# Three transpose banks for part of the band attention, a deferred output norm, and row factors kept in SBUF

## The chip, the core and the metric

The kernel runs on one core of a Trainium2 chip. The metric is the time of one execution in device microseconds (us). A core has a matrix engine (TensorE; PE in the profile, with its weight loads as PEld), a vector engine (VectorE; DVE), an activation engine (ScalarE; ACT), a general engine (GpSimd; POOL) and the queue from which this kernel issues its DMAs (SyncE; SP). Each engine takes its instructions in one fixed order, which is set when the program is built. Matrix products land in PSUM, in banks of 128 x 512 float32 values; working tiles lie in SBUF.

## The reference

One layer of a streaming encoder on 2048 prompt tokens and 32 sample tokens, all in float32. Both attention groups read the same projected input, and their outputs meet in one output projection:

```python
qa, ka, va, qb, kb, vb = split_proj(rmsnorm(hp, g_attn[i]), w_in[i])
oa = diff_attn_prompt(qa, ka, va, t5_table, lam)      # group A: 4 heads, two maps, chunk-causal
ob = band_attn_prompt(qb, kb, vb, band_table[i])      # group B: 8 heads, own chunk and 8 before it
hp = hp + merge(oa, ob, subln_g[i], out_norm_b[i], w_out[i], lam_init)
hp = ffn_ple(hp, p_prompt[i], g_mlp[i], w_up[i], w_down[i], w_ple_gate[i], w_ple_proj[i])

def merge(oa, ob, subln_g, out_norm_b, w_out, lam_init):
    oa = rmsnorm(oa, subln_g, SUBLN_EPS) * (1.0 - lam_init)
    ob = rmsnorm(ob.reshape(B, T, WIDTH_B), out_norm_b)
    return jnp.concatenate([oa.reshape(B, T, WIDTH_A), ob], axis=-1) @ w_out
```

What the change touches is the projection, the band attention (group B) and `merge`: the norm over the 512 columns of `ob`, and the product with `w_out`.

## The kernel before

**Precision.** A float32 operand is split into a high and a low part, and a product is made of three matmuls (`mm3`, lines 219 to 221). The splits are ACT's (high part, line 181) and POOL's or DVE's (low part, lines 166, 176, 187). A weight tile of 512 KB is read, split and then used by a group of 24 matmuls: 8 slices of the contraction, three matmuls each.

**Blocks.** The 2080 tokens form four blocks: 0 to 2 of 512, and 3 of 544 with the sample tokens, which is worked in two halves of 272. Blocks 0 and 1 go through projection, attention, output projection and MLP ahead of blocks 2 and 3.

**Projections** (`proj`). For group B (`grp` 1) and group A (`grp` 0): values per 128 tokens (tile `vps`, 24 matmuls 256 wide, evicted by ACT, line 427), then queries and keys per 128 columns (tile `qps`, 24 matmuls 512 or 272 wide, evicted by DVE, lines 475 and 480). Before, their PSUM tiles go round three banks: `mm` is a ring of two banks of the pool `mz` and one of the pool `mmx`.

**Band attention** (`attn_b`). A head's queries are taken 128 at a time; I call one such tile a band step. With all 640 keys it has four score matmuls in two banks (`sb`, line 804), the bias and maximum on DVE (line 807), the exponential and the scaling on ACT (lines 812, 814, with DVE's small steps 811 and 813 between), five transposes of the weights (`tpb`, line 826) into two tiles of PSUM, their eviction as high and low part by ACT and DVE (`pb`, lines 834, 835), and, once for two steps, the product with the values (`ob`, line 856: six matmuls, evicted at lines 859 to 861). The heads are called in four sets, `JB`: pairs of 256 queries (0, 1), (2, 3), (4, 5) and (6, 7, 8), eight heads each; the first two sets are the first half, `JB[: len(JB) // 2]`. Steps of the first set have fewer keys and two score matmuls each. Banks: two for scores (`ps_s`), two for transposes (`ps_t`), one for outputs (`ps_o`).

**Output norm and projection.** The attention outputs go to memory (`oT`) and come back. `onorm` reads the four group B slices of a block, squares and adds them (ACT lines 875, 877; POOL), and `colnorm2` makes the row factors r from them (two `css` matmuls, ACT lines 1050 to 1052, DVE 1053 to 1056) and stores them in memory (`rB`). `oload` reads r back and all eight slices (`raw_o`, tile `oraw`, a ring of `self.nt` buffers tagged `tmp`), multiplies four of them by gain and r (line 902) and splits them (`oact`). `outproj` then runs eight groups of 24 matmuls (`ops`), one for each 128 output columns, and adds the input (`hd`, line 926).

**Order.** Code order is a priority. A scheduler places each instruction on its engine when it can run by its own estimate, so that matmuls of the band attention stand between those of the projections. `weave` and `weave2` issue one generator's pieces between another's steps. Before, the norms of blocks 0 and 1 are issued within the group A projection of blocks 2 and 3 (`ONP`: from step 28 on), and block 1's `oload` within block 0's output projection, one slice for each of its eight steps (`OW`).

Of the kernel before, what the change touches and what calls it, by code (L numbers as in the profile page):

```python
# [13 lines left out]
F32 = mybir.dt.float32  # L14
# [4 lines left out]
PSUM = bass.MemoryType.PSUM  # L19

P = 128
# [13 lines left out]
BLK = 544  # L35
# [7 lines left out]
HALVES = [(0, 1), (2, 3)]  # L43
# [29 lines left out]
GS = 3  # L73
OW = 1
# [4 lines left out]
ONP = (28, 1, 6)  # L79
ONQ = (8, 1, 1)  # L80
PW = 272


def drain(gen):
    for _ in gen:
        pass


def weave2(main, sides, at):
    n = 0  # L90
    for _ in main:
        for i, side in enumerate(sides):
            if n in (at[0] + i * at[1], at[0] + i * at[1] + at[2]):
                next(side, None)
        n += 1
    for side in sides:
        drain(side)


def weave(main, side, step, i=0, n=1):  # L100
    for _ in main:
        if i % step == 0:
            for _ in range(n):
                next(side, None)
        i += 1
    drain(side)
# [37 lines left out]
class Kern:  # L144
# [14 lines left out]
    def pool_tt(self, out, a, b, op):  # L159
        nc = self.nc  # L160
        if len(out.shape) == 2:
            n = out.shape[1]
            m = -(-n // PW)
            for i in range(m):
# [700 lines left out]
        self.dma(t, self.oT[:, k, t0 : t0 + n])  # L865
        return t

    def onorm(self, b, wk, ps, tag, dst):
        nc = self.nc
        n, t0 = BN[b], 512 * b  # L870
        sq = wk.tile([P, BLK], F32, tag="acc", bufs=2, name="sqacc")[:, :n]
        for k in range(4, 8):
            raw = self.raw_o(wk, k, t0, n)
            if k == 4:
                nc.scalar.activation(sq, raw, AF.Square)
            else:
                nc.scalar.activation(raw, raw, AF.Square)
                self.pool_tt(sq, sq, raw, ALU.add)
        yield from self.colnorm2(sq, b, 1.0 / 512, wk, ps, tag, dst, [])

    def oload(self, b, wk, up, out):
        nc = self.nc
        n, t0 = BN[b], 512 * b
        if isinstance(up, tuple):
            oact = up[0].tile([P, 8, n], F32R, tag="h", name="oact")
            oact = [
                [oact[:, k] for k in range(8)],
                [up[1].tile([P, up[1].aw], F32R, tag="u", name="ou") for _ in range(8)],
            ]
        elif up.whole:  # L890
            oact = [up.tile([P, 8, up.aw], F32R, tag="act", name="oact") for _ in range(2)]
            oact = [[t[:, k, :n] for k in range(8)] for t in oact]
        else:
            oact = [[up.tile([P, up.aw], F32R, tag="u", name="ou")[:, :n] for k in range(8)] for _ in range(2)]
        out[b] = oact
        for k in range(8):
            if k == 4:
                r = wk.tile([P, BLK], F32, tag="r", bufs=2, name="rb")[:, :n]
                self.dma(r, self.rB[:, t0 : t0 + n])
            raw = self.raw_o(wk, k, t0, n)  # L900
            if k >= 4:
                nc.vector.scalar_tensor_tensor(
                    raw, raw, self.g_b[:, k - 4 : k - 3], r, op0=ALU.mult, op1=ALU.mult
                )
            self.split(oact[0][k], oact[1][k], raw, "act", "dve")
            yield
# [473 lines left out]
    def run(self):  # L1380
        tc, nc, a = self.tc, self.nc, self.a
        with ExitStack() as top:

            def opened(stack, name, bufs, space=None, side="left"):
                kw = {} if space is None else {"space": space}
                return stack.enter_context(
                    tc.tile_pool(name=name, bufs=bufs, side=side, reuse_waits="tile", **kw)
                )
# [8 lines left out]
            mm = opened(top, "mm", MM, PSUM)  # L1397
            mmx = ExitStack()
            mm0 = mz = mm
            mm = Rings((mz, "mm"), (mz, "mm"), (opened(mmx, "mmx", 1, PSUM), "mm"))  # L1400
            tp = mm
            psx = ExitStack()
            ps_s = opened(psx, "pss", 4 - MM, PSUM, "right")
            ps_t = opened(psx, "pst", 2, PSUM, "right")
            ps_o = opened(psx, "pso", 1, PSUM, "right")
# [3 lines left out]
            sg = opened(s12, "sg", 2)  # L1409
            self.rb = {}  # L1410
            with ExitStack() as x:
                pp = opened(x, "pp0", 3, side="right")
                wv = opened(x, "wv0", 1, side="right")
                acts = {b: self.actpair() for b in HALVES[0]}
# [20 lines left out]
            pp = opened(ppx, "pp", 1)  # L1435
            self.rawp = Rings((self.wp, "wr"), (opened(ppx, "wr3", 1), "wr"))
            with ExitStack() as x:
                wk = opened(x, "setup", 1, side="right")
# [11 lines left out]
            def lifted(gen):  # L1450
                while True:
                    with tc.high_priority(tc.tile_snap_priority() - mark):
                        done = next(gen, self) is self
                    if done:
                        return
                    yield
# [5 lines left out]
            self.rows(3, sg)  # L1462
            bx = ExitStack()
            bp = opened(bx, "b", 1, side="right")
            for js in JB[: len(JB) // 2]:
                self.attn_b(js, bp, ps_s, ps_t, ps_o)
            weave(self.proj((2,), 1, acts, sg, mm), lifted(self.prep(3, acts, pp, mm, "mm")), 3)
            ppx.close()
            self.rawp = Rings((self.wp, "wr"))
            self.caches(sg, tp)  # L1470
            drain(self.proj((3,), 1, acts, sg, mm))
            wqx = ExitStack()
            wq = opened(wqx, "wq", 1, side="right")
            for js in JB[len(JB) // 2 :]:
                self.attn_b(js, bp, ps_s, ps_t, ps_o)

            def proj_a():
                yield from self.proj(HALVES[1], 0, acts, sg, mm, gs=range(GS))
                for b in HALVES[1]:
                    yield from self.proj((b,), 0, acts, sg, mm, vs=(), gs=range(GS, 4))  # L1480

            weave2(proj_a(), [self.onorm(b, wq, mm, "mm", self.rB) for b in HALVES[0]], ONP)
            s12.close()
            self.small = False
            sq_ = ExitStack()
            actq = Sized(opened(sq_, "actq", 2), 512, True)
            oa = {}
            drain(self.oload(0, wq, actq, oa))
            wqx.close()
            bx.close()  # L1490
            wk = opened(sq_, "wk", 1)
            fk = opened(sq_, "fk", 1)
            hq = opened(sq_, "hq", 1)
            uq = Sized(opened(sq_, "uq", 8), 512)
            self.qpool = opened(sq_, "ak", 1)
            mz = mm
# [7 lines left out]
            acc, cn, st = {}, {}, {}  # L1504
# [3 lines left out]
                yield from self.cnorm(b, wk, act, cn)  # L1508

            acc = {b: [] for b in range(4)}  # L1510
            weave(self.outproj(0, wk, oa[0], mm, acc[0]), self.oload(1, wk, (hq, uq), oa), 1, 0, OW)
            weave(self.outproj(1, wk, oa[1], mm, acc[1]), norms(0, actq, mm), 1, 1)
            up = Sized(opened(top, "uh", 20, side="right"), BLK)
            oxs = ExitStack()
# [7 lines left out]
            for b in HALVES[0]:  # L1522
# [4 lines left out]
                h = hload(hq, 512, b)  # L1527
# [10 lines left out]
            mm = mm0  # L1538
# [8 lines left out]
            wk = opened(top, "wk4", 1, side="right")  # L1547
# [5 lines left out]
            with ExitStack() as x:  # L1553
# [3 lines left out]
                g = self.outproj(3, wk, oa[3], md, acc[3])  # L1557
# [9 lines left out]
            h = hload(hh[0], BLK, 0)  # L1567
            g = self.gate(0, h, up, None, md, wk, made[0], pT)
# [7 lines left out]
            h = box[0]  # L1576
# [3 lines left out]
            g = self.gate(2, h, up, None, md, wk)  # L1580
# [8 lines left out]
            h = box[0]  # L1589
            weave(m, f, 1)  # L1590
            g = self.gate(3, h, up, cs, md)
# [67 lines left out]
```

## Time and profile before

| | before |
|---|---|
| median of three runs | 3063.79 us (3062.14 to 3065.21) |
| the profiled execution | 3069.65 us |
| its span, first to last instruction | 3067.9 us |
| TensorE busy | 2947.2 us (96%) |
| mean granted TensorE clock | 0.985 |
| scores of the band attention (`sb`) on TensorE | from 525.0 to 1231 us |
| last matmul of the projections (`qps`) starts | 773.1 us |
| first matmul of the output projection (`ops`) starts | 825.5 us |

The profile is of one execution. Busy shares count an engine's instructions; matmuls overlap, so a group's busy time is more than the time it takes on a full engine. A wait is the idle time of an engine just ahead of an instruction, with the engine and tile that ended it.

### The profile page before, as it was taken

Reading aid. Unit: us, or ns where it says so; the run is one execution under the profiler, and the core shown is the slowest. Engines: PE = TensorE matmul, PEld = TensorE weight load, DVE = VectorE, ACT = ScalarE, POOL = GpSimd, SP = SyncE. Lnnn points to the kernel's source line nnn. Section 1 sums busy time; section 2 is a strip of 40 time slices with the busy share of each in tenths; the row PEclk is TensorE's granted clock in tenths of the full one; section 3 lists DMA queues with packets and bytes.
Section 4 is the critical chain, followed back from the end, with each engine's and each line's share of the span. In section 5 each row is a group of like instructions: output and inputs, shape, how many; then the busy total and the mean of one; then the engine's idle time right before and its main releaser. Section 6 shows DMA issues by size and latency. Waiting matters only on the chain. (4 is left out here: it accounts for less than half of the span.)

```text
span 3067.9 us, 50404 instructions
## 1 busy us (share of the span) xinstructions
PE 2947.2 (96%) x17409; PEld 2599.0 (85%) x17409; DVE 1830.6 (60%) x4233; ACT 1746.5 (57%) x3234; POOL 1887.9 (62%) x2509
## 2 busy tenths in 40 slices
PE   7999999899789999999999999999899999999997
PEld 6788889899677888888888888879798888999997
DVE  5156554654655555566666565545677885577664
ACT  5256554765666666566666565554555545555455
POOL 3467775324146544656655565777688888787774
PEclk9999999999899999999999999999999999999999
DMA  9878866976687554455655543347433446333331
GB/s 310 250 222 245 241 221 211 262 228 211 190 248 241 147 148 131 145 155 172 198 149 155 150 128 125 118 148 249 136 131 117 148 151 231 122 101 112 102 99 57
DMA packets 298119, 529.54 MB, mean 173 GB/s; under 512 B 36668, under 2 KB 161632, under 8 KB 297864
## 3 DMA queue, kind: packets, MB, share of 16 engines
q1 hardware_dynamic: 297864, 526.32, 55.6%
q8 instruction: 138, 2.26, 0.3%
q14 instruction: 117, 0.96, 0.1%
HBM read 425.19 MB, written 104.97 MB: 173 GB/s over the span
## 5 line engine op out<-in xcount | busy, mean ns | idle before, releaser
L176 POOL TENSOR_TENSOR wl<-wr,wh 128x256 fp32r<-128x256 f32 x648 | 492.8, 792 | 270.2 <-ACT wh L181 230.7
L181 ACT ACTIVATE piece<-wr 128x512 fp32r<-128x512 f32 x406 | 245.8, 625 | 290.4 <-PE ups L220 133.3
L176 POOL TENSOR_TENSOR piece<-wr,piece 128x256 fp32r<-128x256 f32 x404 | 338.0, 863 | 92.3 <-ACT piece L181 85.2
L181 ACT ACTIVATE wh<-wr 128x1024 fp32r<-128x1024 f32 x228 | 240.5, 1055 | 190.8 <-PE ups L220 45.9
L166 POOL TENSOR_TENSOR wl<-wr,wh 128x256 fp32r<-128x256 f32 x264 | 202.9, 799 | 208.4 <-ACT wh L181 202.6
L219 PE MATMUL dps<-uh,piece 128*128 128x272 f32 (+1 forms) x768 | 247.0, 325 | 8.3 <-ACT piece L181 5.0
L221 PE MATMUL dps<-uh,piece 128*128 128x272 f32 (+1 forms) x768 | 247.3, 325 | 1.1 <-POOL piece L166 0.9
L220 PE MATMUL dps<-ul,piece 128*128 128x272 f32 (+1 forms) x768 | 248.1, 324 | 0.1
L166 POOL TENSOR_TENSOR piece<-wr,piece 128x256 fp32r<-128x256 f32 x280 | 235.1, 872 | 18.9 <-ACT piece L181 15.4
L219 PE MATMUL ups<-cs,piece 128*128 128x256 f32 (+1 forms) x864 | 246.2, 285 | 0.0
L221 PE MATMUL ups<-cs,piece 128*128 128x256 f32 (+1 forms) x864 | 246.1, 285 | 0.0
L220 PE MATMUL ups<-cs,piece 128*128 128x256 f32 (+1 forms) x864 | 245.9, 285 | 0.0
L219 PE MATMUL qps<-aH,wh 128*128 128x512 f32 (+1 forms) x640 | 226.9, 355 | 2.0 <-DVE ql L475 2.0
L220 PE MATMUL qps<-aL,wh 128*128 128x512 f32 (+1 forms) x640 | 227.9, 356 | 0.0
L221 PE MATMUL qps<-aH,wl 128*128 128x512 f32 (+1 forms) x640 | 226.5, 354 | 0.0
L1112 DVE TENSOR_TENSOR h<-h,dps 128x512 f32<-128x512 f32 x256 | 173.5, 682 | 80.2 <-PE dps L221 77.0
L638 ACT ACTIVATE e<-e,nm 128x128 f32<-128x128 f32 (+16 forms) x136 | 157.2, 1156 | 108.5 <-DVE nm L636 108.0
L1155 DVE TENSOR_TENSOR h<-h,dps 128x272 f32<-128x272 f32 (+1 forms) x384 | 189.0, 514 | 42.9 <-PE dps L221 42.3
L219 PE MATMUL dps<-uh,wh 128*128 128x512 f32 x512 | 205.7, 402 | 0.6 <-DVE h L1112 0.6
L219 PE MATMUL ups<-cH,wh 128*128 128x512 f32 x512 | 202.5, 396 | 0.0
L221 PE MATMUL ups<-cH,wl 128*128 128x512 f32 x512 | 202.2, 395 | 0.1
L220 PE MATMUL ups<-cL,wh 128*128 128x512 f32 x512 | 202.0, 394 | 0.0
(307 smaller groups left out, 9234.0 us busy)
## 6 DMA issues: line engine op xcount, KB each, us to landing
wr<-w_up SPq DMA_DIRECT2D x128, 512.0 KB, 3.5
wr<-w_down SPq DMA_DIRECT2D x128, 512.0 KB, 3.6
v<-vSa SPq DMA_DIRECT2D x64, 512.0 KB, 4.6
q<-qS SPq DMA_DIRECT2D x128, 256.0 KB, 5.2
wr<-w_qk SPq DMA_DIRECT2D x50, 512.0 KB, 5.2
ka<-kS SPq DMA_DIRECT2D x32, 512.0 KB, 7.1
wr<-w_out SPq DMA_DIRECT2D x32, 512.0 KB, 4.8
wr<-w_ple_gate SPq DMA_DIRECT2D x32, 512.0 KB, 3.5
```

The source lines that it names most:

```text
L166: nc.gpsimd.tensor_tensor(out[:, sl], a[:, sl], b[:, sl], op=op)
L176: nc.gpsimd.tensor_tensor(out[:, sl], a[:, sl], b[:, sl], op=op)
L181: nc.scalar.activation(hi, raw, AF.Copy)
L219: nc.tensor.matmul(ps, lh, rh, start=start and i == 0, stop=False)
L220: nc.tensor.matmul(ps, lh, rl, start=False, stop=False)
L221: nc.tensor.matmul(ps, ll, rh, start=False, stop=stop and i == n - 1)
L638: nc.scalar.activation(row, row, AF.Exp, bias=nmx, accum_out=z[:nr, m : m + 1])
L1112: nc.vector.tensor_tensor(hv, hv, ps, op=ALU.add)
L1155: nc.vector.tensor_tensor(hv, hv, ps, op=ALU.add)
```

## The change

Four edits, in one diff:

- The band attention's first half (sets 0 and 1) transposes into a ring of three banks: the two of `ps_t` and the one of `mmx`. From there on the projections of blocks 2 and 3, and the preparation of block 3, use the two banks of `mz` alone.
- Only block 0's norm is still issued within the group A projection. Block 1's is issued within block 0's output projection: its first piece after step 3, its second after step 5 (`O1`, `O2`). It reads its four slices in one DMA into a tile of the pool `hq`, and adds them up in one of `uq`, not in the `tmp` and `acc` rings.
- Block 1's `oload` begins after step 5 and issues three slices for each step (`O3`), in place of one from step 0 on.
- r of blocks 0 and 1 stays in the SBUF tile that `colnorm2` made; it isn't stored to `rB` and read back. Blocks 2 and 3 are as before.

```diff
+O1, O2, O3 = 3, 5, 3
-    def onorm(self, b, wk, ps, tag, dst):
+    def onorm(self, b, wk, ps, tag, dst, out=None, room=None):
         nc = self.nc
         n, t0 = BN[b], 512 * b
-        sq = wk.tile([P, BLK], F32, tag="acc", bufs=2, name="sqacc")[:, :n]
+        if room is None:
+            sq = wk.tile([P, BLK], F32, tag="acc", bufs=2, name="sqacc")[:, :n]
+        else:
+            room, sq = room
+            sq = sq.tile([P, sq.aw], F32, tag="u", name="sqacc")[:, :n]
+            room = room.tile([P, 8, n], F32, tag="h", name="oraws")[:, :4]
+            self.dma(room, self.oT[:, 4:8, t0 : t0 + n])
         for k in range(4, 8):
-            raw = self.raw_o(wk, k, t0, n)
+            raw = self.raw_o(wk, k, t0, n) if room is None else room[:, k - 4]
...
-        yield from self.colnorm2(sq, b, 1.0 / 512, wk, ps, tag, dst, [])
+        yield from self.colnorm2(sq, b, 1.0 / 512, wk, ps, tag, dst, [] if out is None else out)
-    def oload(self, b, wk, up, out):
+    def oload(self, b, wk, up, out, r=None):
...
-            if k == 4:
+            if k == 4 and r is not None:
+                r = r.pop()
+            elif k == 4:
                 r = wk.tile([P, BLK], F32, tag="r", bufs=2, name="rb")[:, :n]
                 self.dma(r, self.rB[:, t0 : t0 + n])
...
-            mm = Rings((mz, "mm"), (mz, "mm"), (opened(mmx, "mmx", 1, PSUM), "mm"))
+            third = opened(mmx, "mmx", 1, PSUM)
+            mm = Rings((mz, "mm"), (mz, "mm"), (third, "mm"))
...
+            tb = Rings((ps_t, "tp"), (ps_t, "tp"), (third, "mm"))
             for js in JB[: len(JB) // 2]:
-                self.attn_b(js, bp, ps_s, ps_t, ps_o)
-            weave(self.proj((2,), 1, acts, sg, mm), lifted(self.prep(3, acts, pp, mm, "mm")), 3)
+                self.attn_b(js, bp, ps_s, tb, ps_o)
+            weave(self.proj((2,), 1, acts, sg, mz), lifted(self.prep(3, acts, pp, mz, "mm")), 3)
...
-            drain(self.proj((3,), 1, acts, sg, mm))
+            drain(self.proj((3,), 1, acts, sg, mz))
...
-                yield from self.proj(HALVES[1], 0, acts, sg, mm, gs=range(GS))
+                yield from self.proj(HALVES[1], 0, acts, sg, mz, gs=range(GS))
                 for b in HALVES[1]:
-                    yield from self.proj((b,), 0, acts, sg, mm, vs=(), gs=range(GS, 4))
-            weave2(proj_a(), [self.onorm(b, wq, mm, "mm", self.rB) for b in HALVES[0]], ONP)
+                    yield from self.proj((b,), 0, acts, sg, mz, vs=(), gs=range(GS, 4))
+            ro = {b: [] for b in HALVES[0]}
+            weave2(proj_a(), [self.onorm(0, wq, mm, "mm", None, ro[0])], ONP)
...
-            drain(self.oload(0, wq, actq, oa))
+            drain(self.oload(0, wq, actq, oa, ro[0]))
...
-            weave(self.outproj(0, wk, oa[0], mm, acc[0]), self.oload(1, wk, (hq, uq), oa), 1, 0, OW)
+            g = self.onorm(1, wk, mm, "mm", None, ro[1], (hq, uq))
+            for i, _ in enumerate(self.outproj(0, wk, oa[0], mm, acc[0])):
+                if i in (O1, O2):
+                    next(g, None)
+                if i == O2:
+                    g = self.oload(1, wk, (hq, uq), oa, ro[1])
+                if i >= O2:
+                    for _ in range(O3):
+                        next(g, None)
+            drain(g)
```

The scheduler makes a new order of this. On TensorE, at the end of the projections, before (names end in a buffer number; `kbt_6457` holds the keys of the last head of band set 1, `x2` is two equal matmuls):

```order
L219 MATMUL qps_12209<-aH_4781,wh_12171 128x272
L220 MATMUL qps_12209<-aL_4782,wh_12171 128x272
L221 MATMUL qps_12209<-aH_4781,wl_12172 128x272
L1046 MATMUL css_12244<-sh_11920,ones_r_118 128x512
L1047 MATMUL css_12244<-sl_11921,ones_r_118 128x512
L804 MATMUL sb_6468<-kbt_6457,q_6460 128x320 x2
L804 MATMUL sb_6472<-kbt_6457,q_6460 128x320 x2
L856 MATMUL ob_6355<-pb_6305,vbt_6192 128x512 x4
L856 MATMUL ob_6355<-pb_6305,vbt_6192 128x2x128
L826 MATMUL tpb_6381<-ident_111,eb_6330 128x128 x4
```

Nothing but band steps follows, up to the second head of band set 2 (`kbt_8433`), where the output projection begins:

```order
L804 MATMUL sb_8541<-kbt_8433,q_8436 128x320 x2
L804 MATMUL sb_8545<-kbt_8433,q_8436 128x320 x2
L826 MATMUL tpb_8456<-ident_111,eb_8403 128x128 x4
L219 MATMUL ops_16133<-oact_12272,wh_16124 128x512
L219 MATMUL ops_16185<-oact_12272,wh_16176 128x512
```

Changed, the same place on TensorE (`kbt_8705` holds the keys of the fourth head of band set 2):

```order
L222 MATMUL qps_12186<-aH_4781,wl_12149 128x272
L1055 MATMUL css_12221<-sh_11920,ones_r_118 128x512
L1056 MATMUL css_12221<-sl_11921,ones_r_118 128x512
L805 MATMUL sb_8716<-kbt_8705,q_8708 128x320 x2
L805 MATMUL sb_8720<-kbt_8705,q_8708 128x320 x2
L857 MATMUL ob_8603<-pb_8553,vbt_8440 128x512 x4
L857 MATMUL ob_8603<-pb_8553,vbt_8440 128x2x128
L827 MATMUL tpb_8629<-ident_111,eb_8578 128x128 x4
L857 MATMUL ob_8603<-pb_8553,vbt_8440 128x2x128
L827 MATMUL tpb_8636<-ident_111,eb_8578 128x128
L220 MATMUL ops_16095<-oact_12236,wh_16086 128x512
L220 MATMUL ops_16134<-oact_12236,wh_16125 128x512
```

What moved: 16 band steps (176 score matmuls stand ahead of the last `qps` before, 240 now, four for a step) went from behind the projections into them. Between the last `qps` and the first `ops` stand 48 score matmuls, 12 band steps, before, and four, one band step, now.

On SP, the DMA queue, at block 1's `oload` within block 0's output projection, before (`hd` is the input that the output projection adds, `hS` its result):

```order
L157 DMA oraw_16262<-oT_87 128x512
L157 DMA hd_16275<-x_t 128x512
L157 DMA wr_16455<-w_out 128x1024
L157 DMA hS_88<-hd_16275 128x512
L157 DMA oraw_16308<-oT_87 128x512
L157 DMA hd_16321<-x_t 128x512
L157 DMA wr_16503<-w_out 128x1024
L157 DMA hS_88<-hd_16321 128x512
L157 DMA oraw_16356<-oT_87 128x512
```

Changed:

```order
L158 DMA oraw_16370<-oT_87 128x512
L158 DMA oraw_16374<-oT_87 128x512
L158 DMA wr_16546<-w_out 128x1024
L158 DMA oraw_16378<-oT_87 128x512
L158 DMA wr_16598<-w_out 128x1024
L158 DMA hd_16391<-x_t 128x512
L158 DMA vbt_8984<-vSb_86 128x8x128
L158 DMA oT_87<-t1_8711 64x512
L158 DMA hS_88<-hd_16391 128x512
L158 DMA oraw_16424<-oT_87 128x512
L158 DMA oraw_16428<-oT_87 128x512
```

What moved: the eight reads stood one to a step of the output projection, and stand now in pairs and threes towards its end. The reads of `rB` and the stores to it, two each, are gone, and block 1's norm reads once instead of four times: seven DMAs fewer in all. Every compute engine has the same instructions as before, in another order.

## Prediction

> **What bounds the kernel now.** I read the page's first part, then the busy time of each engine by stretches, then TensorE's waits in the stretches that have any.
>
> ```profile
> PE 2947.2 (96%) x17409; PEld 2599.0 (85%) x17409; DVE 1830.6 (60%) x4233; ACT 1746.5 (57%) x3234; POOL 1887.9 (62%) x2509
> ```
>
> TensorE is busy for 96% of the span, no other engine for more than 62%. So nothing is won by faster work elsewhere, only by stretches in which TensorE stands idle or runs at a low clock. The stretches around the change (start and end in us, length, busy us of each engine, granted clock, share and rate of the DMAs):
>
> ```profile
> 525.00:650.00 125.00, 115.80 (x861) 109.97 (x862) 74.65 (x293) 86.50 (x213) 30.75 (x59) 0.99 0.88 251
> 650.00:773.30 123.30, 123.30 (x801) 113.61 (x800) 57.33 (x204) 72.31 (x145) 56.17 (x87) 1.00 0.70 212
> 773.30:825.40 52.10, 34.99 (x146) 26.16 (x145) 28.86 (x108) 33.91 (x71) 7.26 (x15) 0.77 0.66 192
> 825.40:1000.00 174.60, 158.29 (x758) 130.08 (x758) 100.19 (x280) 110.45 (x209) 89.18 (x128) 0.96 0.81 238
> 1000.00:1950.00 950.00, 947.83 (x4886) 800.06 (x4885) 575.14 (x1472) 582.05 (x968) 534.20 (x753) 1.00 0.50 149
> ```
>
> From 650 to 773.3 TensorE is full at clock 1.00. Then the projections are over, and until 825.4, when the output projection begins, band steps run alone: 35.0 of 52.1 us busy, at clock 0.77. No engine is full there (ACT 33.9, DVE 28.9 us): a chain of dependent instructions sets the pace. What ended TensorE's idle time there (tile and releaser: us, count, the longest):
>
> ```profile
> PE ob L856 <- DVE pb L835: 7.3, 3, 6.6
> PE sb L804 <- DVE stb L807: 7.0, 11, 0.9
> PE tpb L826 <- DVE pb L835: 2.4, 2, 1.6
> ```
>
> Eleven score tiles waited 0.64 us each for a bank that DVE reads (7.0/11). The long wait of 6.6 us is a different matter; the timeline shows it (start, length, and in brackets the idle time before it):
>
> ```profile
> 792.95 0.63 ACT L877 ACTIVATE oraw<-oraw 128x512 f32<-128x512 f32 x1 [7.21 <-DMA oraw<-oT]
> 795.65 1.65 PE L856 MATMUL ob<-pb,vbt 128*128 128x512 f32 x3 [6.64 <-DVE pb L835]
> ```
>
> ACT stood 7.21 us before a square of the output norm, whose slice had not landed, with the band step's exponential behind it; TensorE ran dry.
>
> **Term 1, the lonely band steps.** By the order, 176 score matmuls of the band stood before the projections' last `qps`, and 240 stand there now; between it and the first `ops` there were 48 (12 steps of four), and now 4. The third transpose bank lets the scheduler run ahead with later steps. No instruction of an engine is saved: the 12 steps now lie between projection matmuls, where they cost what TensorE needs for them. That price is taken from the stretch in which they did so before (TensorE's busy us and instructions of one tile at a time: `sb`, `tpb`, `ob`, in this order, each in both stretches, then `qps`):
>
> ```profile
> 650.00:773.30 123.30, 16.18 (x78) 1.00 0.70 212
> 773.30:825.40 52.10, 12.95 (x48) 0.77 0.66 192
> ...
> 650.00:773.30 123.30, 14.16 (x100) 1.00 0.70 212
> 773.30:825.40 52.10, 11.77 (x59) 0.77 0.66 192
> ...
> 650.00:773.30 123.30, 13.29 (x60) 1.00 0.70 212
> 773.30:825.40 52.10, 14.22 (x36) 0.77 0.66 192
> ...
> 650.00:773.30 123.30, 98.85 (x562) 1.00 0.70 212
> ```
>
> The work of the lonely stretch at the prices of the full one: 48 × 16.18/78 + 59 × 14.16/100 + 36 × 13.29/60 = 9.96 + 8.35 + 7.97 = 26.3 us. Matmuls overlap: the four tiles' busy times add up to 142.5 us in a stretch of 123.3, so I scale by 123.3/142.5 = 0.865 and have 22.7 us. Out of 52.1 us that leaves a gain of 29.4, if the steps slip in without new waits.
>
> **Term 2, new waits in the projections.** Two things speak for some. First, blocks 2 and 3 now go round two banks, not three. A bank must be evicted while the other is filled:
>
> ```profile
> 641.21 0.28 PE L219 MATMUL vps<-wh,aH 128*128 128x256 f32 x1
> 642.16 0.28 PE L221 MATMUL vps<-wh,aL 128*128 128x256 f32 x1
> ...
> L427 ACT ACTIVATE vraw<-vps,rcol x68: 446/459/494, 20.6 to 649.3; 128x256 f32<-128x256 f32 x64, 32x256 f32<-32x256 f32 x4
> L475 DVE SCALAR_TENSOR_TENSOR ql<-qps,rbt x40: 422/677/693, 90.2 to 766.9; 128x512 f32<-128x512 f32 x24, 128x272 f32<-128x272 f32 x16
> ```
>
> The two `vps` rows lie eight matmuls apart, 0.95 us, so a group of 24 takes 24 × 0.119 = 2.85 us, the shortest there is. The eviction takes 0.46 us on ACT, or at most 0.69 on DVE (shortest, median, longest in ns). That leaves some 2.4 us for the eviction to be late behind band work on its engine, ahead of which one more group stood before. Second, the band steps are now denser: 78/4 = 19.5 steps in the last 123.3 us before, 6.3 us a step; now 64/4 = 16 more, in a stretch longer by 16 × 22.7/12 = 30.3 us, so 35.5 steps in 153.6 us, 4.3 us a step. The lonely steps ran at 52.1/12 = 4.3 with their long stall, 3.8 without it (45.5/12; 6.6 us taken off). So the new pace is within what the chain has run at, with little to spare. The waits of the projections so far, from 372 us, where TensorE's order begins to differ, to 773:
>
> ```profile
> PE sb L804 <- DVE stb L807: 5.8, 4, 2.2
> PE vps L220 <- POOL wl L176: 2.0, 1, 2.0
> PE o L696 <- ACT pH L689: 1.8, 1, 1.8
> PE s L623 <- DVE e L630: 1.6, 2, 1.2
> PE sb L804 <- DMA q<-qS: 1.0, 1, 1.0
> PE tpb L826 <- DVE pb L835: 1.0, 1, 1.0
> PE sb L804 <- DMA vbt<-vSb: 0.3, 1, 0.3
> ```
>
> That is 13.5 us in 400, 6.8 of it at band tiles behind DVE (`sb`, `tpb`), and not one wait for an eviction (ACT `vraw`, DVE `ql`). From below the cost is 0. From above: blocks 2 and 3 have 36 `vps` and 48 `qps` groups; if each waited as the lonely `sb` did, 0.64 us, 84 × 0.64 = 54. I take 10: the 6.8 us of band waits once more for twice as many steps, and five evictions late by 0.64 (3.2). It is near the lower end because no eviction was waited for so far.
>
> **Term 3, the output projection of block 0.** The stretch from 825.4 to 1000 has 174.6 − 158.3 = 16.3 us idle. Its longest waits, and the one behind the longest:
>
> ```profile
> PE ops L219 <- DVE stb L813: 6.3, 1, 6.3
> PE sb L804 <- DVE stb L807: 4.2, 2, 2.2
> PE ops L219 <- ACT oact L181: 1.4, 1, 1.4
> ...
> 869.92 0.63 ACT L181 ACTIVATE oact<-oraw 128x512 fp32r<-128x512 f32 x1 [7.11 <-DMA oraw<-oT]
> 872.77 0.76 PE L219 MATMUL ops<-oact,wh 128*128 128x512 f32 x1 [6.33 <-DVE stb L813]
> ```
>
> ACT stood 7.11 us at block 1's `oload` before a slice that had not landed; the band's exponential, and behind that DVE's sum, were queued after it, and TensorE was dry for 6.3. `oload(1)` now starts after step 5, so this wait at its old place goes. What comes in: two `css` matmuls, 0.8 us by the row of a 512-wide `ops` below; four squares of 0.63 us on ACT (2.5 us, beside 110 of 175 busy); the additions on POOL (89 of 175 busy); one read of 1 MB; and three slices of `oload` a step in place of one. The nearest transfers (KB each, us to landing), and block 0's 64 `ops` of the low part (ns, and first and last start):
>
> ```profile
> oraw<-oT SPq DMA_DIRECT2D x36, 256.0 KB, 3.5
> y_t<-h SPq DMA_DIRECT2D x6, 1024.0 KB, 4.3
> ...
> L220 PE MATMUL ops<-oact,wh x64: 387/390/776, 826.5 to 896.1; 128*128 128x512 f32 x64
> ```
>
> From 825.5 to 896.1 lie eight steps of 8.8 us. So the norm's read of 4.3 us, its squares and its row factors, issued after steps 3 and 5, have two to four steps. `oload`'s eight slices, issued three at a time after steps 5, 6 and 7, are covered less: three reads in a row are 10.5 us, and block 1's first group wants all eight within its 8.8. Bounds: −16, if all idle time goes, and +15, two stalls of 7.1. I take −4: the 6.3 goes, 2.3 comes new. If ACT stands at a slice there, band exponentials wait behind it, and TensorE's scores behind those.
>
> **At nothing.** r isn't stored and read back: seven DMAs fewer on SP with the four slices in one, none of them a releaser in the rows above. Block 1's norm leaves the projections, where ACT had time (72.3 of 123.3 us). One of its late slices could be the cause of the 7.2 us stall, which is in term 1 already. From 1000 to 1950 TensorE idles 2.2 us in 950, and after about 2030 us its order is the same: what is won before is not lost there.
>
> **Sum.** −29.4 + 10 − 4 = −23.4 us. The profiled execution took 3069.65 us, so 3046.2; it lies 5.9 above the median of 3063.79, so the median comes to 3040.4, and I say 3040.
>
> **The rivals.** *A, the bank that the projections lost.* Slower: each of the 84 groups waits 0.64 us for the eviction. 3063.8 − 29.4 − 4 + 54 = 3084. It decides from 33.4/84 = 0.40 us a group. For it: ACT evicts `vps` and runs the band's exponentials, at 77% when denser (33.9/12 = 2.8 us of ACT a step; 35.5 × 2.8 = 100, and 72.3 − 19.5 × 2.8 = 17 of other work: 117 of 153.6). Against: no wait for an eviction so far, and 2.4 us of slack. 9%.
>
> *A′, the clock goes with the banks.* Frequent short gaps while groups go round two banks bring the projections' clock down, as the lonely steps had 0.77 with a third of the time idle. From 525 to 773.3, 248.3 us at 0.77 are 248.3/0.77 − 248.3 = 74 more: 3040.4 + 74 = 3114. Against: 525 to 650 had 9.2 us idle at 0.99. 2%. The Trainium skill states this as a rule in "TensorE: Matmul & The Clock Gate", section "A second HAM failure mode: psum-queue depth-cycling": short idles between matmul groups that cycle through PSUM banks made the clock swing between half and full. By that rule the change would lose; the trace agrees for the lonely stretch (0.77), not for the projections (0.99 and 1.00).
>
> *B, the chain sets the end.* The band steps keep their own pace and the projections wait for them: 4.3 us a step and 17/35.5 = 0.5 of ACT's other work make 4.8; 35.5 × 4.8 = 170 against 153.6, so 17 us, and 20 to 25 with the evictions of term 2 and some stalls. In place of the 10 that makes 3063.8 − 29.4 − 4 + 20 to 25 = 3050 to 3055. For it: the 3.8 us a step. Against: projection matmuls don't depend on the band; they only stand behind it in the order. 20%.
>
> *C, no new waits, and the output projection's idle goes.* 3063.8 − 29.4 − 16 = 3018. 13%.
>
> *D, block 1's output projection starves.* The bunched slices land late twice: 3063.8 − 29.4 + 10 + 15 = 3059. For it: the 10.5 us against 8.8, and two stalls of 7 us at reads of `oraw` before. Against: reads overlap, and the first six go out a step or two ahead. 6%.
>
> That the change doesn't do what it says is excluded by the rows of the order: the steps stand among the projections.
>
> **How the numbers follow.** The forecast has 50%. About 0.2%, 6.1 us, can be told from no change, so faster is below 3057.7 and slower above 3069.9. Of the forecast's 50, 49 are faster and 1 is the same; of C's 13 all are faster; B's 20 divide into 13, 4 and 3; D's 6 into 2, 3 and 1; A and A′ are 11 slower. Faster 0.77, same 0.08, slower 0.15. The range goes from C's 3018, less 2 of the runs' spread (3062 to 3065), to 3062, which takes in B and D, and leaves out A, A′ and the worst of B and some of C.
>
> **What would show it.** Right: from the last `qps` to the first `ops` 2 to 8 us, at a clock near 1.00; the last `qps` starts some 20 to 33 us later, at about 793 to 806; no ACT wait of 7 us for `oraw` at the squares or at `oload(1)`; waits of `vps` for ACT, `qps` for DVE and `sb` for DVE under 25 us in all from 372 on. Wrong: `qps` waits for `ql`, or `vps` for `vraw`, by dozens (A), with a clock under 0.95 (A′); `sb` waits for `stb` of more than 20 us in the projections (B); the first `ops` of block 1 behind `oact` by 7 us or more (D). If TensorE's gap shrinks by 29 and the whole does not, the time is lost after 825, and term 3 is what failed.

## The result and the profile after

| | before | changed |
|---|---|---|
| median of four runs | 3064.5 us (3062.14 to 3065.92) | 3036.18 us (3031.87 to 3036.98) |
| the profiled execution | 3069.65 us | 3036.97 us |
| its span | 3067.9 us | 3035.2 us |
| last `qps` | 773.1 us | 796.1 us |
| first `ops` | 825.5 us | 799.8 us |
| first `ups` (MLP of blocks 0 and 1) | 965.4 us | 938.1 us |
| last `ups` of blocks 0 and 1 | 1961.5 us | 1935.7 us |
| first `ops` of block 2 | 2050.8 us | 2020.0 us |

The ratio is 0.9904, with a 95% interval of 0.989 to 0.9918: 28 us faster, where 23 were forecast.

The stretches of the changed kernel, cut where those of before were cut (start and end, length, busy us of TensorE, its weight loads, DVE, ACT and POOL, granted clock, DMA share and rate):

```profile
525.00:650.00 125.00, 116.70 (x869) 110.81 (x870) 77.94 (x303) 89.87 (x218) 32.60 (x61) 0.99 0.88 261
650.00:796.40 146.40, 146.40 (x958) 135.13 (x957) 88.57 (x323) 106.19 (x217) 54.39 (x89) 1.00 0.76 222
796.40:799.80 3.40, 3.01 (x17) 2.15 (x16) 3.37 (x10) 3.40 (x8) 1.93 (x3) 1.00 0.95 255
799.80:974.40 174.60, 159.87 (x741) 129.81 (x740) 100.02 (x276) 113.26 (x212) 97.62 (x138) 0.94 0.82 247
974.40:1950.00 975.60, 968.27 (x4958) 814.30 (x4957) 580.77 (x1464) 585.62 (x975) 550.36 (x780) 1.00 0.48 147
```

The stretch of lonely band steps has shrunk from 52.1 to 3.4 us, at clock 1.00. The full stretch ahead of it has grown from 123.3 to 146.4 and is still full: ACT is busy for 73% of it where it was 59%. The stretch of the output projections hasn't gained: 14.7 us idle where 16.3 were, at a clock of 0.94 where it was 0.96. From 974 to 1950 the idle time is 7.3 us, where 2.2 were in an equally long stretch from 1000 on.

TensorE's busy time in the full stretch, for `sb`, `tpb` and `ob` apart:

```profile
650.00:796.10 146.10, 31.23 (x132) 1.00 0.76 222
...
650.00:796.10 146.10, 24.88 (x160) 1.00 0.76 222
...
650.00:796.10 146.10, 21.82 (x96) 1.00 0.76 222
```

54 score matmuls, 60 transposes and 36 of `ob` more than before. At the prices of the prediction these are (11.2 + 8.5 + 8.0) × 0.865 = 23.9 us; the stretch grew by 23.1.

TensorE's waits from 372 to 810 us, the longest first:

```profile
PE sb L805 <- DMA q<-qS: 4.0, 3, 1.7
PE tpb L827 <- DVE pb L836: 2.0, 2, 1.2
PE ob L857 <- ACT eb L813: 1.4, 1, 1.4
PE qps L220 <- DVE ql L476: 1.4, 1, 1.4
PE s L624 <- DVE e L631: 1.2, 2, 0.6
PE vps L220 <- ACT vraw L428: 0.8, 1, 0.8
```

The two evictions that are now waited for cost 2.2 us together. All waits of the list come to 12.9 us, four short ones below these included; before, they were 13.5 up to 773 us, with the waits of the lonely stretch still to come. What the prediction named as signs of being right came: a gap of 3.7 us at clock 1.00, the last `qps` 23 us later, no long ACT wait for `oraw` (at most 3.1 us, from 372 us to the end of the output projections, where 7.2 and 7.1 stood before), and 2.7 us of waits of `vps` for ACT and of `qps` and `sb` for DVE, where up to 25 were allowed.

### The profile page after: what moved, and what is told of

It reads as the page before. It is cut to its first block, busy times and chain, and to the rows that moved or that the text cites. A ratio compares the mean times of both kernels' runs of the same rounds, so it can differ in the third digit from the quotient of the medians.

```text
span 3035.2 us, 50381 instructions
## 1 busy us (share of the span) xinstructions
PE 2936.1 (97%) x17409; PEld 2590.1 (85%) x17409; DVE 1825.3 (60%) x4233; ACT 1746.3 (58%) x3234; POOL 1886.8 (62%) x2509
```

## The experiments

Each kernel was timed in turn with the kernel before on the same chip; the ratio is against that. "Lost" is the idle time of a stretch and, of its busy time, the share by which the granted clock lies under 1: from 773.3 to 825.4 before, 17.1 + 35.0 × 0.23 = 25.2 us.

**The banks alone.** The first edit on the kernel before:

```diff
             for js in JB[: len(JB) // 2]:
-                self.attn_b(js, bp, ps_s, ps_t, ps_o)
+                self.attn_b(js, bp, ps_s, tb, ps_o)
...
-            drain(self.proj((3,), 1, acts, sg, mm))
+            drain(self.proj((3,), 1, acts, sg, mz))
...
```

> The kernel before with the bank edit alone (three transpose banks for the first half of the band attention, two banks for the projections of blocks 2 and 3); norms, oload and the store of r as before. By the order 236 of the band's score matmuls now stand ahead of the last qps (before: 176) and 4 between it and the first ops (before: 48). Theory 1, that of the prediction: the third bank closes the stretch of lonely band steps; the gap from the last qps to the first ops is under 8 us and the time is 3036 to 3045. Theory 2: the stretch was block 0's output projection waiting for block 1's norm, which needs the whole first half of the band; the third bank brings that half's end forward, so the gap closes here too, 3036 to 3045. Rival A (two banks starve the projections): 3084, or no gain. If the time stays within 6 us of 3064, the bank edit did nothing for the whole.

Ratio 0.9942 (0.9925 to 0.9959), 3044.97 us: some 18 us faster, not 28. The gap and the stretch of the output projections:

```profile
794.80:797.40 2.60, 2.18 (x16) 1.73 (x14) 1.95 (x8) 2.49 (x5) 0.79 (x2) 1.00 0.83 256
797.40:946.40 149.00, 133.31 (x618) 110.11 (x619) 83.29 (x225) 87.57 (x163) 72.79 (x105) 0.93 0.79 237
```

The gap is 2.6 us (last `qps` 794.8, first `ops` 797.4), but the stretch of the output projections is 149.0 us long, where the changed kernel has 138.3.

**The norm alone.** The other edits without the first:

```diff
             for js in JB[: len(JB) // 2]:
-                self.attn_b(js, bp, ps_s, tb, ps_o)
+                self.attn_b(js, bp, ps_s, ps_t, ps_o)
-            weave(self.proj((2,), 1, acts, sg, mz), lifted(self.prep(3, acts, pp, mz, "mm")), 3)
+            weave(self.proj((2,), 1, acts, sg, mm), lifted(self.prep(3, acts, pp, mm, "mm")), 3)
...
```

> The changed kernel with the bank edit undone (two transpose banks, projections on three), so block 1's late norm from memory of its own, the late oload and r in SBUF alone. By the order 176 score matmuls stand ahead of the last qps, as in the kernel before, but only 4 between it and the first ops. Theory 1 (the third bank makes the gain, the norm is worth the 4 us of term 3): the lonely steps come back in another place, 3055 to 3062. Theory 2 (block 0's output projection waited for block 1's norm): the gap closes without the third bank, the 11 steps run among ops matmuls at about 1.9 us each, 3036 to 3045. Between the two: the steps paced by two banks at 4.3 us keep ops waiting, about 3050.

Ratio 1.0018 (1.0008 to 1.0028): a little slower than the kernel before. Two rows of its stretches, the gap and the output projections:

```profile
768.60:771.40 2.80, 2.80 (x21) 2.55 (x19) 1.76 (x6) 2.61 (x5) 1.47 (x2) 1.00 0.93 210
771.40:927.40 156.00, 140.41 (x641) 113.15 (x640) 88.33 (x257) 98.99 (x187) 73.99 (x114) 0.92 0.79 244
```

The gap has closed here too, without the third bank, and the time has not gained: the output projections now lose 15.6 + 140.4 × 0.08 = 26.8 us, and the rest of what the gap had cost is lost behind them, most of it once the band is done (13.7 us idle from 1250 to 1954). The third bank isn't needed to end the stretch, which theory 1 of the first run had as its doing. Theory 2 falls, since ending it isn't a gain by itself. What theory 1 of this run said did come, the lonely steps in another place, but the gain of 4 us that it left to the norm did not.

**The lost bank alone.** The projections of blocks 2 and 3 on two banks, the transposes on two as before:

```diff
-            drain(self.proj((3,), 1, acts, sg, mm))
+            drain(self.proj((3,), 1, acts, sg, mz))
...
-                yield from self.proj(HALVES[1], 0, acts, sg, mm, gs=range(GS))
+                yield from self.proj(HALVES[1], 0, acts, sg, mz, gs=range(GS))
...
```

> The kernel before with the projections of blocks 2 and 3 (and the preparation of block 3) on two PSUM banks; the third is given to nobody in that stretch but the norms' row sums. This is the cost of the lost bank by itself. Term 2 of the prediction took part of 10 us for it, 3 us for five late evictions: 3064 to 3068. Rival A: 84 groups by 0.64 us, about 3118. If it costs nothing: within 2 us of the kernel before, and no TensorE wait for vraw or ql beyond the ones of before.

Ratio 0.9944 (0.9928 to 0.9961), 3046.71 us: no loss but a gain of some 17 us, which no theory had. The stretches of the full projections and of the lonely steps, and the waits from 372 us to the last `qps` that are for an eviction:

```profile
637.30:765.30 128.00, 127.84 (x820) 116.92 (x818) 61.40 (x217) 78.28 (x156) 57.59 (x88) 1.00 0.70 210
765.30:809.00 43.70, 31.60 (x146) 23.42 (x145) 28.67 (x106) 31.99 (x68) 7.26 (x15) 0.87 0.79 229
```

```profile
PE qps L219 <- DVE ql L475: 1.4, 1, 1.4
...
PE vps L219 <- ACT vraw L427: 0.8, 1, 0.8
...
PE qps L219 <- ACT vraw L427: 0.2, 1, 0.2
```

Two banks are enough: 2.4 us of waits over 84 groups, and the projections run at a clock of 1.00. The lonely stretch is still there, but 43.7 us long: the square of the norm (line 877) that ACT stood 7.2 us at waits 1.5 us here. The last `vps` is 8.8 us earlier too (637.3 for 646.1); 3.7 of these lie ahead of all differences in the order and so between two executions (the ACT instruction shown further below starts at 360.57 here, at 364.32 before). The scheduler's order differs in many small places on all engines, on TensorE from 374 us on; which of them made the other 5 isn't settled.

Beside this run the banks alone say less than they seemed to. They differ from it by one thing, the third bank for the transposes. It moves 15 steps into the projections (236 score matmuls ahead of the last `qps`, here 176) and brings the gap from 43.7 to 2.6 us, and yet the times, 3044.97 and 3046.71 us, can't be told apart.

**A shared bank.** The changed kernel with the projections on all three banks, so that they and the transposes take the third in turn:

```diff
-            drain(self.proj((3,), 1, acts, sg, mz))
+            drain(self.proj((3,), 1, acts, sg, mm))
...
```

> The changed kernel, but the projections of blocks 2 and 3 keep three banks: the third is shared between them and the band's transposes, in turn. By the order 340 score matmuls stand ahead of the last qps (changed kernel: 240), 2 in the gap. If the lost bank costs nothing and TensorE is full in the projections, more steps ahead move work and save none: 3033 to 3040, first ops some 45 us later than in the changed kernel. If idle time of the output projection comes from band chains standing in it, fewer steps there make it faster: 3025 to 3033. If transposes and projections wait for each other at the shared bank: 3045 or more.

Ratio 1.0318 (1.03 to 1.0336), 3160.67 us: 100 us slower. The first two rows of its stretches, up to the last `vps`, which comes at 834 (changed kernel: 646):

```profile
372.00:470.70 98.70, 58.33 (x246) 44.63 (x247) 50.61 (x143) 45.36 (x88) 26.38 (x40) 0.69 0.34 92
470.70:834.30 363.60, 331.74 (x2146) 288.84 (x2147) 194.96 (x720) 225.75 (x496) 110.91 (x188) 0.97 0.71 212
```

From 372 to 834 some 100 us are lost (40.4 + 18.1 and 31.9 + 10.0), where the kernel before loses about 16 up to its last `vps`: most of what the whole got slower. In the first of the two TensorE waits for both attention groups, 12.4 us of it for one load of q, and no projection matmul stands in between to fill it. That the turns of the ring tie the two streams together is the likely reason; it wasn't tried apart from the order that came with it.

**The kernel before again**, for a second profile.

> The kernel before, unchanged, for a second profile. The sum of the prediction was made against one profiled execution in which two reads of oraw were late (ACT idle 7.2 and 7.1 us, TensorE idle 6.6 and 6.3). Theory 'fixed': the stalls belong to the program, the stretch from the last qps to the first ops is 51 to 53 us again, with some 25 us lost in it to idle time and a low clock. Theory 'chance': they belong to that execution; the stretch is 44 to 47 us, and the execution some 6 to 13 us shorter than the one before.

Ratio 1.0009 (0.9995 to 1.0022). Its lonely stretch, and the wait in it behind the late square:

```profile
774.60:826.40 51.80, 35.88 (x149) 27.57 (x147) 28.99 (x109) 33.93 (x71) 7.28 (x15) 0.73 0.68 194
```

```profile
PE ob L856 <- DVE pb L835: 6.1, 3, 5.5
```

The stretch and its stall belong to the program: the sum rested on a typical execution.

**The changed kernel again.**

> The changed kernel, unchanged, for a second profile beside the others of this call. Ratio 0.990 again (0.988 to 0.992). First ops at 797 to 802, last qps 2 to 5 us ahead of it. The 4.6 us wait of the output projection that stands behind a late read of hd, and the half clock after it, come back if they belong to the program and not if the first execution was unlucky.

Ratio 0.9907 (0.9882 to 0.9931); last `qps` at 800.1, first `ops` at 803.9, about 2 us later than expected with the gap as expected. The stall of the output projection is there again (5.1 us).

**The norms one step later**, `ONP` 29 for 28 in the kernel before.

> The kernel before with the norms of blocks 0 and 1 issued one step later within the group A projection; nothing else. It does the same work with the same banks, and the count of score matmuls ahead of the last qps and in the gap is the same (176, 48). It measures how far the scheduler's order alone moves the time. If the gain of 14 us that two banks for the projections gave by themselves is a matter of how the scheduler's order happens to fall, this moves by several us too (more than 5 either way); if small edits of the order cost nothing, it stays within 3 us of the kernel before, and the 14 us are due to the banks.

Ratio 1.0004 (0.9994 to 1.0015). But the edit moved nothing: in the two traces every engine has the same instructions in the same order as in the kernel before, buffer numbers left out. So this is the kernel before a third time (last `qps` 774.9, first `ops` 825.5), and whether the 17 us of the lost bank come from the banks or from how the order happens to fall stays untested.

**r through memory.** The changed kernel without its fourth edit:

```diff
-            weave2(proj_a(), [self.onorm(0, wq, mm, "mm", None, ro[0])], ONP)
+            weave2(proj_a(), [self.onorm(0, wq, mm, "mm", self.rB)], ONP)
...
-            drain(self.oload(0, wq, actq, oa, ro[0]))
+            drain(self.oload(0, wq, actq, oa))
...
```

> The changed kernel with r of blocks 0 and 1 stored to memory and read back, as before; banks and late norm as changed. The prediction put this edit at nothing: 3033 to 3041. If block 0's first ops waits for the round trip of r (a store and a read, some 4 us each, behind the norm), first ops moves from 799.8 to 808 or so and the time to 3044.

Ratio 0.9926 (0.9902 to 0.995), which overlaps the changed kernel's; first `ops` at 798.6, no later. The round trip isn't waited for at the first `ops`; a few us of the whole can't be excluded.

**A ring of its own.** The kernel before; only the buffers of block 1's norm slices differ:

```diff
-            weave2(proj_a(), [self.onorm(b, wq, mm, "mm", self.rB) for b in HALVES[0]], ONP)
+            weave2(proj_a(), [self.onorm(b, wq, mm, "mm", self.rB, b * 2) for b in HALVES[0]], ONP)
...
-        t = wk.tile([P, BLK], F32, tag="tmp", bufs=self.nt, name="oraw")[:, :n]
+        t = wk.tile([P, BLK], F32, tag="tq" if own else "tmp", bufs=own or self.nt, name="oraw")[:, :n]
...
```

> The kernel before; only block 1's norm reads its four slices into a ring of two buffers of its own, not into the tmp ring that block 0's oload uses. Position of the norm, banks and r as before. Theory: in the kernel before, block 0's first ops waits since its last slices stand in the tmp ring behind block 1's norm slices, and these need the whole first half of the band. Then the gap from the last qps to the first ops closes to 3 to 5 us here (by the order 4 score matmuls stand in it), with banks as before. If closing the gap is itself what gains, 3036 to 3045. If the band's pace with two banks then holds the output projection, as in the run with the norm alone, 3055 to 3068.

Ratio 1.0011 (1.0002 to 1.0021). The gap and the stretch of the output projections:

```profile
772.60:775.40 2.80, 2.80 (x20) 2.55 (x19) 1.76 (x6) 2.64 (x5) 1.51 (x2) 1.00 1.00 213
775.40:965.40 190.00, 162.69 (x760) 129.89 (x759) 110.99 (x344) 123.27 (x238) 75.07 (x115) 0.94 0.77 224
```

This is the cleanest of the runs: two buffers end the lonely stretch, and nothing is gained. The output projections end at 965.4, where the three executions of the kernel before have 965.4, 970.2 and 969.3, since their stretch is 190.0 us long in place of 140. They lose 27.3 + 162.7 × 0.06 = 37.1 us. Before, the gap lost 25.2 and the output projections, by the row below, 13.5 + 126.5 × 0.03 = 17.3, together 42.5; so 37.1 of the 42.5 are lost again.

```profile
825.40:965.40 140.00, 126.49 (x607) 103.88 (x607) 80.80 (x224) 85.47 (x161) 68.62 (x100) 0.97 0.83 241
```

The lonely steps have gone among the `ops`, and there TensorE waits for them as it did alone (the longest row of its waits from 775 to 990 us):

```profile
PE sb L804 <- DVE stb L807: 19.6, 15, 5.2
```

What held the first `ops` is seen in the kernel before. The end of its lonely stretch, on SP's queue and on ACT:

```profile
817.84 0.46 SPq L157 DMA_DIRECT2D oT<-t  x1
820.09 1.28 SPq L157 DMA_DIRECT2D oraw<-oT  x3
822.80 0.63 ACT L877 ACTIVATE oraw<-oraw 128x512 f32<-128x512 f32 x1 [1.13 <-DMA oraw<-oT]
824.52 1.14 ACT L181 ACTIVATE oact<-oraw 128x512 fp32r<-128x512 f32 x2
```

The last output of the first half goes to memory; block 1's last norm slice is read and squared; block 0's last slices, issued with it, are split; 1 us later `ops` begins. Block 0's `oload` stood behind block 1's norm in the `tmp` ring, and that norm needs the whole first half of the band. That the gap is 2.8 us with a ring of its own shows it.

**Late, from the old rings.** The changed kernel without memory of its own for the norm:

```diff
-            g = self.onorm(1, wk, mm, "mm", None, ro[1], (hq, uq))
+            g = self.onorm(1, wk, mm, "mm", None, ro[1])
```

> The changed kernel, with block 1's late norm reading its slices into the tmp ring and adding up in the acc ring, not in memory of its own. Theory 'place': what matters is that the norm is issued behind block 0's oload; 3033 to 3041, gap 3 to 5 us. Theory 'memory': slices of the norm stand in the tmp ring between hd and tmp of block 0's output projection and hold it up; the gap is 3 to 5 us all the same, but the stretch of the output projections grows from 138 us to 145 or more, 3042 or later.

Ratio 0.9912 (0.9896 to 0.9929): as the changed kernel. Both signs came: the whole as 'place' had it, the stretch of the output projections as 'memory' had it (149.9 us, by 225.2 for 242.6 in the stretch behind, to the end of the band). Memory of its own isn't what gains.

**Slices spread**, `O1, O2, O3 = 1, 3, 2` for 3, 5, 3.

> The changed kernel with block 1's norm after steps 1 and 3 (changed: 3 and 5) and its oload from step 3 on at two slices a step (changed: from step 5 at three). If the bunched slices of oload are what TensorE waits for at the start of block 1's output projection (2.5 us behind oraw in both profiles, and the low clock after), this wait goes: 3028 to 3034. If its cover is enough either way, 3034 to 3040. If the earlier slices crowd the tmp ring and hd, later: over 3042.

Ratio 0.9911 (0.9894 to 0.9927). The wait for `oraw` went, and others came to the same: no difference that can be told.

**hd in a ring of its own**, two buffers for blocks 0 and 1 of the changed kernel:

```diff
-            h = wk.tile([P, BLK], F32, tag="tmp", bufs=self.nt, name="hd")[:, :n]
+            h = wk.tile([P, BLK], F32, tag="hd" if b < 2 else "tmp", bufs=2 if b < 2 else self.nt, name="hd")[:, :n]
```

> The changed kernel; hd of blocks 0 and 1 (the input that the output projection adds) takes two buffers of its own, not the tmp ring. In both profiles of the changed kernel TensorE stands 4.6 and 5.1 us before an ops whose weights ACT splits late, since DVE waits 6.8 us for hd. If hd is issued late because of the ring, both go with the low clock after: 3028 to 3033. If hd is late because the DMA engines are full there (share 1.03 to 1.08 from 820 to 840), nothing changes: 3034 to 3040.

Ratio 0.9875 (0.986 to 0.9891), 3027.86 us (3025.12 to 3034.94): the fastest of all, though its interval touches the changed kernel's. The reason given for it isn't borne out: its profile still has the wait,

```profile
PE ops L220 <- DVE hd L935: 5.5, 1, 5.5
```

with DVE 8.8 us at a late hd. The profiled execution was the slowest of its four, 3034.94 us, so where the faster ones gain is open.

## Why the prediction held, and which terms were off

The profiled executions differ by 32.7 us. Of this 3.3 arise ahead of the first place where an engine's order differs, and are no work of the change: over the runs with the same order up to there, the instruction below starts between 359.68 and 364.73. The same instruction before and after:

```profile
364.32 1.06 ACT L181 ACTIVATE aH<-xt 128x1024 fp32r<-128x1024 f32 x1 [2.13 <-DVE xt L382]
```

```profile
361.00 1.06 ACT L182 ACTIVATE aH<-xt 128x1024 fp32r<-128x1024 f32 x1 [2.11 <-DVE xt L383]
```

The other 29.4 stand against a forecast of 23.4. From these rows to the last `qps` 408.8 us became 435.1 (+26.3); the gap 52.4 became 3.7 (−48.7); from the first `ops` to the end 2242.4 became 2235.4 (−7.0). Sixteen steps moved ahead of the last `qps`: eleven out of the gap and five out of the stretches behind it, 1.9 us each at the prediction's price (22.7/12). The column "measured" takes this price for the moved steps, so it divides the whole by an estimate:

| term | forecast | measured | working |
|---|---|---|---|
| 1, lonely steps | −29.4 | −27.8 | −48.7 + 11 × 1.9 |
| 2, new waits in the projections | +10 | −4 | 26.3 − 16 × 1.9 |
| 3, from the output projection on | −4 | +2.5 | −7.0 + 5 × 1.9 |

**Term 1, right in size by this cut, but not shown to be what gained.** "The third transpose bank lets the scheduler run ahead with later steps": the banks alone do put 236 score matmuls ahead of the last `qps` and close the gap. But the stretch was there because block 0's `oload` stood behind block 1's norm in the `tmp` ring. Either edit ends it, the banks by finishing the first half of the band sooner (block 1's last norm slice is squared at 767.6 us with the banks alone, at 822.8 before), the late norm by freeing the ring. What the prediction did see is that the price of the place to which the steps go counts. Within full projections sixteen steps made 26.3 us, 1.6 us each for the 1.9 forecast; among the `ops` of block 0 they keep their own pace, and the time comes back as waits (the ring of its own: 50 us longer there).

That the third bank gains by this isn't shown, though. Going from run to run, two banks for the projections made the kernel some 17 us faster (0.9944), the third bank for the transposes nothing more that can be told (0.9942), and the norm edit with r some 11 more (0.9904 and 0.9907). The prediction had a loss of 3.2 us (the late evictions), a gain of 22.6 (29.4 less the 6.8 of band waits) and a gain of 4 in these places. So its total was met in part by luck. In another sequence the parts may come out otherwise: the changed kernel with its transposes on two banks, which would tell what the third bank is worth there, wasn't run.

One reading was off as well. The prediction says that none of the seven DMAs that went is a releaser in its rows; but the slice behind the stall of 7.21 us is one of block 1's norm slices, whose four reads became one.

**Term 2, mis-sized.** I took 10 from bounds of 0 and 54; it was −4. The evictions were about as supposed (2.2 us for 3.2), but the band's waits didn't double with its pace: those behind DVE or ACT at band tiles (`sb`, `tpb`, `ob`) come to 4.8 us with the short ones, where they were 6.8. The step that failed is to scale these waits with the number of steps. The run with two banks shows the lost bank free of cost, so rival A is out. It was even faster, which the bounds left out; why stays open. A′ is out too: the clock of the projections was 1.00 with two banks. What the Trainium skill tells of another kernel in "TensorE: Matmul & The Clock Gate", section "A second HAM failure mode: psum-queue depth-cycling", a clock that swings because TensorE idles briefly between matmul groups that go round PSUM banks, was not met in these projections; groups last 2.85 us or more, and hardly one of them was followed by idle time.

**Term 3, too large, and lost again behind.** The output projections themselves went from 140.0 to 138.3 us, with 72 score matmuls in them as before: 1.7 us for the 4 forecast. The five steps came out of the stretch behind, up to the last `ups`, which still became no shorter (996.6 and 998.0 us); the prediction had put that stretch at nothing, and the cause is open. The wait of 6.3 us went, as said. In its place stands one of 4.6, which I hadn't named: DVE stands late at hd, the band's small step and ACT behind it, and ACT's split of the weights behind that, just ahead of the `ops` at 844.48:

```profile
841.35 0.69 DVE L935 TENSOR_TENSOR hd<-hd,ops 128x512 f32<-128x512 f32 x1 [6.78 <-DMA hd<-x_t]
842.13 0.63 ACT L940 ACTIVATE tmp<-hd 128x512 f32<-128x512 f32 x1 [6.60 <-DVE stb L814]
843.38 1.99 ACT L182 ACTIVATE wh<-wr 128x1024 fp32r<-128x1024 f32 x2
```

And the low clock behind a stall, which the sum had no term for, costs more than before (0.94 for 0.96). The edits belong together: banks alone make the stretch 149.0 us long, the norm edit on top 138.3, and the whole goes from 18 us faster to 28. On the kernel before, the same norm edit gains nothing. So the two edits don't add, 0 and 18 making 28, and the sum's habit of pricing one by one would have missed this, had both been predicted alone.

B is out (the band's chain is waited for less than before in the projections), C's 3018 wasn't reached since the output projection kept its waits, and D was 2.5 us at one slice, not 15.

## What to carry to other kernels

Before pricing the work that fills a slow stretch, find what ends the stretch: follow the first instruction behind it back through its buffers, not only its data; a ring shared by two users makes one wait for the other's inputs. Ending such a stretch is not a gain by itself: where its work is waited for in the new place too, the idle time goes along with it. Price it by the new place. A total that comes out right doesn't show that its terms do: try the edits one on top of the other. And take an engine's spare buffer to be worth nothing until a wait for it is seen: here three banks were no faster than two.

## What the hardware did that was not expected

The clock can fall behind a single stall of a few us. TensorE in the changed kernel, first behind the wait of 4.6 us, then 6 us later, and the granted clock (the last but two of the numbers) of both stretches:

```profile
844.48 0.80 PE L220 MATMUL ops<-oact,wh 128*128 128x512 f32 x1 [4.61 <-ACT wh L182]
...
847.20 0.63 PE L220 MATMUL ops<-oact,wh 128*128 128x512 f32 x1
847.63 0.63 PE L221 MATMUL ops<-oact,wh 128*128 128x512 f32 x1
...
851.13 0.40 PE L220 MATMUL ops<-oact,wh 128*128 128x512 f32 x1
851.37 0.39 PE L221 MATMUL ops<-oact,wh 128*128 128x512 f32 x1
...
844.40:850.20 5.80, 5.72 (x14) 0.50 0.57 186
850.20:860.00 9.80, 9.80 (x50) 1.00 0.76 221
```

Equal matmuls start 0.43 us apart up to 850.2, and 0.23 to 0.24 apart from there on. Some thirteen of them at 0.2 us more make 2.6 us, so by this the stall cost 7.2 us, not the 4.6 that the list of waits shows. This is no fixed price. Behind the wait of 6.3 us of the kernel before, the clock was at 0.50 for 3.4 us (872.7 to 876.1); behind one of 2.5 us in the changed kernel it was 0.51 over the next 6.3 us (from 874.7), and behind one of 2.0 us, at 2140.6, it stayed at 1.00.
